# Three column tiles of gate weights split ahead, the second token half two tiles later, and the transfers and masks of the first FFN moved to its down stage

## The chip, the cores and the metric

The kernel runs on one core of a Trainium2 chip. The metric is the device time of one execution in microseconds (us), as the median of several runs. The engines are TensorE (PE in the profile; PEld is its weight load), VectorE (DVE), ScalarE (ACT), GpSimd (POOL) and SyncE (SP), each with an instruction stream of its own that it works off in order. SP's queue issues most transfers between memory and the chip; POOL issues the accumulating ones, each of which is an instruction in POOL's stream.

## The reference, cut to what matters

A decoder trunk with two layers on a sequence of 1024 tokens with 1024 features. Each layer is an FFN, a mixer and a second FFN, with a normalisation before and after each:

```
def swiglu(x, wg, wu, wd):
    return (jax.nn.silu(x @ wg) * (x @ wu)) @ wd

for layer in range(DEPTH):                       # DEPTH = 2
    f = swiglu(rmsnorm(h, ffn_pre_g[layer, 0]), ffn_w_gate[layer, 0], ffn_w_up[layer, 0], ffn_w_down[layer, 0])
    h = h + 0.5 * rmsnorm(f, ffn_post_g[layer, 0])
    m = rmsnorm(h, mix_pre_g[layer])
    m = hybrid_mixer(m, ...) if layer % 2 == 0 else stick_breaking(m, ...)
    h = h + rmsnorm(m, mix_post_g[layer])
    f = swiglu(rmsnorm(h, ffn_pre_g[layer, 1]), ffn_w_gate[layer, 1], ffn_w_up[layer, 1], ffn_w_down[layer, 1])
    h = h + 0.5 * rmsnorm(f, ffn_post_g[layer, 1])
```

The FFN's inner width is D_FF = 1408, eleven column tiles of 128. All is float32.

## The kernel before

**Stages.** Six stages follow one another: FFN, mixer, FFN, and the same in layer 1. The tokens are held as two halves of 512. Float32 products are made from two parts of each operand: a rounded one (fp32r) and the rest. A split is one ACT instruction (`L336` for weights, `L276` for others, CAST) and one DVE subtraction (`L337`, `L277`); a product is three matmuls (`mm3`, `L287` to `L289`). The large products use Strassen's scheme, so they need sums and differences of blocks of the operands.

**The gate and up products (`gu`).** Loop 1 runs over the eleven column tiles `c` of the gate weights. For each it loads the tile (`rawt`), splits its two halves (`wq`: `w0`, `w1`) and makes a quarter product of four times three matmuls, `w0` with the first token half (`quarter`, into `pa`); ACT copies the result to `ph`. The other quarter product (`a12`, with `w1`) runs a tile or two later, accumulates in the same bank, and ACT applies Silu to it (`L414`). At the tiles 2 to 5 `second_half` transposes the rows of the second token half on PE (`xps`, `L327`, eight transposes per call), which ACT copies out (`xr`, `L329`); at the tiles 4 to 7 `combos` makes the sums of Strassen's scheme on DVE (`L388` to `L397`). `pin` keeps the matmuls of the first six tiles in the order of the program; elsewhere a scheduler sets each engine's order when the kernel is built. Loop 2 runs over the eleven tiles again with the remaining five quarter products (`pb`, `pc`, `pd`, the last two used twice), the weight combinations made on POOL (`blocks`, `L421` to `L424`).

**Jobs.** `jobs` are steps on POOL's queue that a later stage needs: sums of weight blocks in memory, made by transfers that copy or accumulate (`Blocks.sums`, line `L82`), and, in the first FFN, the masks of the mixer (`mask_steps`, `L168` to `L187`). In the first FFN `job(0)` issues three steps in each tile of loop 1 after the third: 8 of masks and 16 of the sums `vsum`, for the value projection of the mixer. `job(1)` issues the sums for the down products (`dsum`) and for the mixer's output projection (`wsum`) in loop 2, as do the later FFNs for theirs.

**The down stage (`down_strassen`).** Seven products (`da` to `de`) of row tiles; each needs rows from memory (`rawd`) and splits. POOL makes the sums of `ph` (`L715`, `L725`). Then comes the epilogue of each token half: the residual rows `h` are loaded, the square sum goes from ACT (`junk`, `ss`) by DVE (`ms`, `L232`) to POOL, which makes its inverse root (`rs`, `L234`), and DVE scales the rows (`L248`). They go into the next stage's transposes.

**What is split ahead.** `first_weights` is called at the end of each stage, before the epilogue of the second token half, and gives `begun_w`, the next stage's first split weights: for an FFN column tile 0, two splits (`gate_weights(..., 0)`). The raw buffers (`rp`) are four, those of split weights (`wp`) six; both are shared by all the stages.

Of the kernel before, what the change touches and what calls it, by code (L numbers as in the profile page):

```python
# [24 lines left out]
NF = DFF // P  # L25
# [64 lines left out]
class Trunk:  # L90
# [263 lines left out]
    def gu(self, cx, wg, wu, A, xn1, gname, gi, jobs, begun):  # L354
# [11 lines left out]
        def second_half(part):  # L366
            R.update(self.make_raw(xn1, gname, gi, xr, [part, part + 4], pin))
            if part < 3:
                return
            self.hctx.close()  # L370
            self.foctx.close()
            rows["sx"] = self.dyn(s4, "sx", 4, side="right")
            rows["t2"] = self.dyn(s4, "t2p", 2, side="right")
# [23 lines left out]
            tt(out=a21, in0=a21, in1=lo(j + 4), op=ALU.add)  # L397

        ph, second = [], []
        pin = self.tc.keep_in_program_order  # L400
        paces = 3, -(-len(jobs[1]) // NF)

        def job(loop):
            for f in jobs[loop][:paces[loop]]:
                f()
            del jobs[loop][:paces[loop]]


        def a12():

# [5 lines left out]
        def blocks(c):  # L416
# [7 lines left out]
            gt(out=b21, in0=b21, in1=t2, op=ALU.subtract)  # L424
            return {"t1": b11, "t2": t2, "t3": b12, "t4": b21, "b22": b22}

        for c in range(NF):

            self.pin_mm = pin if c < 6 else None
            h = [self.ph.tile([P, TB], F32, name="ph%d" % tb, tag="ph") for tb in range(2)]  # L430
            w0, w1 = begun if begun and c == 0 else self.gate_weights(wg, c)
            ps = self.acc.tile([P, TB], F32, name="pa", tag="acc")
            self.quarter(ps, w0, A[0:4], True, True)
            nc.scalar.copy(out=h[1], in_=ps)
            while len(second) > (c < 8):
                a12()
            second.append((ps, w1, h))
            ph.append(h)
            if 2 <= c <= 5:
                second_half(c - 2)  # L440
            if 4 <= c <= 7:
                combos(c - 4)
            if c > 2:
                job(0)

        B = blocks(0)
        W = [self.split_w(B[n]) for n in ("t2", "t3")]
# [8 lines left out]
        for c in range(NF):  # L456
            h = ph[c]
            if c:
                B = blocks(c)
            pb = self.acc.tile([P, TB], F32, name="pb", tag="acc")  # L460
            pc = self.acc.tile([P, TB], F32, name="pc", tag="acc")
            pd = self.acc.tile([P, TB], F32, name="pd", tag="acc")
            if c == NF - 1:
                pe = self.acc.tile([P, TB], F32, name="pe", tag="acc")
                pf = self.acc.tile([P, TB], F32, name="pf", tag="acc")
            u2 = h[1]
            last = c == NF - 1
            self.quarter(pb, W[0] if c == 0 else self.split_w(B["t2"]), S[2], True, True)
            tt(out=u2, in0=pb, in1=u2, op=ALU.add)
            self.quarter(pc, W[1] if c == 0 else self.split_w(B["t3"]), S[3], True, True)  # L470
            c22 = tm.tile([P, TB], F32, name="c22", tag="c22")
            tt(out=c22, in0=pc, in1=u2, op=ALU.add)  # L472
            self.quarter(pd, W[2] if c == 0 else self.split_w(B["t1"]), S[1], True, True)
            c21 = tm.tile([P, TB], F32, name="c21", tag="c21")
            c12 = tm.tile([P, TB], F32, name="c12", tag="c12")
            if last:

                self.quarter(pe, self.split_w(B["t4"]), A22, True, True)
                self.quarter(pf, self.split_w(B["b22"]), S[4], True, True)
                tt(out=c12, in0=pd, in1=u2, op=ALU.add)  # L480
                tt(out=c21, in0=pe, in1=c22, op=ALU.add)
                tt(out=c22, in0=pd, in1=c22, op=ALU.add)
                nc.scalar.activation(out=c21, in_=c21, func=AF.Silu)
                tt(out=c12, in0=pf, in1=c12, op=ALU.add)
            else:
                tt(out=c22, in0=pd, in1=c22, op=ALU.add)
                w4, w3 = self.split_w(B["t4"]), self.split_w(B["b22"])
                self.quarter(pc, w4, A22, False, True)
                tt(out=c21, in0=pc, in1=u2, op=ALU.add)
                nc.scalar.activation(out=c21, in_=c21, func=AF.Silu)  # L490
                self.quarter(pd, w3, S[4], False, True)
                tt(out=c12, in0=pd, in1=u2, op=ALU.add)
            tt(out=h[0], in0=h[0], in1=c12, op=ALU.mult)
            tt(out=h[1], in0=c21, in1=c22, op=ALU.mult)
            if c > NF // 2:
                self.down_sums(ph, c - 1 - NF // 2)
            job(1)
        tmp.close()
        s4.close()
        return ph  # L500
# [110 lines left out]
    def ffn(self, l, f, x0, xn1, hsrc, hdst, last):  # L611
        a = self.a
        wg, wu, wd = a["ffn_w_gate"][l, f], a["ffn_w_up"][l, f], a["ffn_w_down"][l, f]
        cx = ExitStack()
        self.ph = self.dyn(cx, "ph", 2 * NF)
        self.s1 = []

        sums = lambda *sets: [step for steps in zip(*[B.sums(T) for B, T in sets]) for step in steps]
        down = self.down_blocks(l, f), self.wd[l, f]
        jobs = [], []  # L620
        if l + f == 0:
            jobs = self.mask_steps() + sums((self.value_blocks(0), self.tv)), sums(down, (self.out_blocks(0), self.td))
        elif l == 0:
            jobs = [], sums(down, (self.value_blocks(1), self.tv))
        elif f == 0:
            jobs = [], sums(down)
        ph = self.gu(cx, wg, wu, x0, xn1, "ffn_pre_g", 2 * l + f, jobs, self.begun_w)
        self.open_fo()
        pg = self.load_pg(a["ffn_post_g"][l, f])
        nxt = ("mix_pre_g", l) if f == 0 else ("ffn_pre_g", 2 * (l + 1))  # L630
        r = self.down_strassen(wd, self.wd[l, f], ph, pg, hsrc, hdst, None if last else nxt)
        cx.close()
        self.hctx.close()
        return r
# [13 lines left out]
        gt(out=z, in0=x, in1=z, op=ALU.subtract)  # L648
        self.s1.append(s1)

    def down_strassen(self, w, T, ph, pg, hsrc, hdst, nxt):
        nc = self.nc
        tt = nc.vector.tensor_tensor
        gt = nc.gpsimd.tensor_tensor
# [68 lines left out]
            tt(out=u2[t], in0=pb[t], in1=u2[t], op=ALU.add)  # L723
        for j in range(KH):
            gt(out=ph[j + KH][0], in0=ph[j][0], in1=ph[j + KH][0], op=ALU.subtract)  # L725

        cp = [pair("c22") for _ in range(2)]
        c22 = [cp[t // 2][:, t % 2] for t in range(NTT)]
# [5 lines left out]
        for t in range(NTT):  # L734
            c = fo[t][:, C[1]]
# [4 lines left out]
        a, b, ks = last_k(1, 1)  # L740
# [7 lines left out]
        for t in range(NTT):  # L748
            c = fo1[t][1]
# [896 lines left out]
    def build(self):  # L1646
        a = self.a
        self.ot = [[self.dram.tile([P, S], F32, name="otd%d_%d" % (l, k)) for k in range(KD)] for l in range(2)]
        self.vd = self.dram.tile([S, D], F32, name="vrows")

        self.sd = [self.dram.tile([P, 4 * TB], F32, name="osum%d" % j) for j in range(3)]
        self.tv, self.td = [{n: self.dram.tile([4 * P, TB], F32, name="%s%d" % (nm, n)) for n in (1, 2, 3, 4)}
                            for nm in ("vsum", "wsum")]
        self.wd = {(l, f): {n: self.dram.tile([NF // 2 * P, TB], F32, name="dsum%d%d_%d" % (l, f, n))
                            for n in (1, 2, 3, 4)} for l in range(2) for f in range(2)}
        self.gg = [self.dram.tile([P, S], F32, name="ggd%d" % h) for h in range(4)]
        for h in self.xn0:
            self.normed(h, h)
        x0 = self.make_first_x(self.xn0, "ffn_pre_g", 0, self.xp)
        x1 = self.first_x(1)  # L1660
        for h in x1:
            self.normed(h, h)
        src = a["x"][0]
        n = 0
        self.begun_w = self.pin_mm = None
        stages = [(l, step) for l in range(2) for step in ("f0", "mix", "f1")]
        firsts = [(lambda l=l: self.row_weights(lambda j: self.value_blocks(l).src(j, 0))) if step == "mix" else
                  (lambda l=l, f=int(step[1]): self.gate_weights(a["ffn_w_gate"][l, f], 0)) for l, step in stages]
        for l in range(2):
            for step in ("f0", "mix", "f1"):  # L1670
                self.first_weights = (firsts + [None])[stages.index((l, step)) + 1]
                last = l == 1 and step == "f1"
                dst = self.out[0] if last else self.new_h(n)
                n += 1
                if n == 2:
                    self.gate_consts()
                if step == "mix":
                    x0, x1 = self.mixer(l, x0, x1, src, dst)
                else:
                    x0, x1 = self.ffn(l, int(step[1]), x0, x1, src, dst, last)  # L1680
                src = dst
        self.foctx.close()
        self.fctx.close()
# [28 lines left out]
```

## Time and profile before

| what | value |
|---|---|
| median of 3 runs (lowest, highest) | 2486.64 us (2486.34, 2493.13) |
| the profiled execution | 2488.17 us, span 2486.2 us |
| TensorE clock granted, mean | 0.985 |
| DVE, ACT, POOL busy | 74%, 46%, 29% of the span |
| first PE work of loop 1 in the four FFNs (`pa`) | 16.6, 937.4, 1284.9, 2140.1 us |
| first PE work of loop 2 (`pb`) | 89.8, 1015.6, 1358.5, 2217.5 us |
| first PE work of the down stage (`da`) | 251.0, 1170.2, 1514.9, 2368.9 us |

The profile is of one execution; its times count from the start of the span. A row of a timeline gives the start in us, the duration in us, the engine, the line, the operation, what it writes and reads, and, in brackets, how long the engine was idle before it and what ended that. Rows that follow one another on PE overlap, since matmuls are pipelined. A row of the waits gives the engine and line that waited, what it waited for, then the us in total, the number of times and the longest. A row of a table of stretches gives the stretch, its length, the busy us of PE, PEld, DVE, ACT and POOL with the number of instructions, the granted clock, the busy share of the transfer engines and GB/s.

### The profile page before, as it was taken

To read this page: it belongs to the slowest core of one execution; us is meant where nothing else is said; L and a number is where in the kernel's file an instruction comes from. 1 tells how busy PE (TensorE), PEld (TensorE's weight loads), DVE (VectorE), ACT (ScalarE), POOL (GpSimd) and SP (SyncE) were. 2 spreads that over 40 slices of the span, in tenths; PEclk is the share of its full clock that TensorE was granted. 3 is DMA by queue.
4 is the path that set the end of the run, shared out by engine and by line. 5 is a ranking of instruction groups with operands and counts; after the bars stand their busy time and mean duration, and the time that the engine had idled before them with its cause. 6 is when DMAs were issued, how large, how long until landed. Compare 5 with 4: busy or idle time off the path is not lost. (4 is left out here: it accounts for less than half of the span.)

```text
span 2486.2 us, 31734 instructions
## 1 busy us (share of the span) xinstructions
PE 2352.8 (95%) x11165; PEld 1925.0 (77%) x11165; DVE 1840.1 (74%) x2877; ACT 1141.2 (46%) x2285; POOL 723.4 (29%) x729
## 2 busy tenths in 40 slices
PE   7999999999888898999989999999999999799998
PEld 6778877777677776877768878778888878588886
DVE  7768789387577778678688677785767677786777
ACT  6323456332466666423456225463333345652343
POOL 3547210011011111567022563110332430234520
PEclk9999999999999998999999999999999999899999
DMA  8867444411112463767454743355574244532234
GB/s 240 229 154 187 141 148 155 143 52 68 60 60 77 150 222 108 194 151 180 140 184 125 162 118 123 122 167 180 126 185 104 90 131 163 176 85 76 73 110 170
DMA packets 278407, 343.64 MB, mean 138 GB/s; under 512 B 13972, under 2 KB 190312, under 8 KB 277736
## 3 DMA queue, kind: packets, MB, share of 16 engines
q1 hardware_dynamic: 251352, 261.39, 33.6%
q0 software_dynamic: 26896, 80.22, 14.2%
q8 instruction: 88, 1.44, 0.2%
q14 instruction: 71, 0.58, 0.1%
HBM read 292.28 MB, written 124.78 MB: 168 GB/s over the span
## 5 line engine op out<-in xcount | busy, mean ns | idle before, releaser
L234 POOL TENSOR_TENSOR rs<-ms,nhalf 128x1 f32<-128x1 f32 (+1 forms) x136 | 103.7, 769 | 839.6 <-DVE ms L232 728.7
L336 ACT CAST wq<-rawt 128x512 fp32r<-128x512 f32 x264 | 163.3, 622 | 362.6 <-PE pc L289 181.9
L337 DVE TENSOR_TENSOR wq<-rawt,wq 128x512 fp32r<-128x512 f32 x264 | 246.5, 938 | 41.9 <-ACT wq L336 37.9
L276 ACT CAST hl<-rawd 128x512 fp32r<-128x512 f32 x212 | 130.7, 620 | 212.0 <-PE dc L289 63.9
L277 DVE TENSOR_TENSOR hl<-rawd,hl 128x512 fp32r<-128x512 f32 x212 | 155.4, 737 | 81.6 <-ACT hl L276 81.5
L287 PE MATMUL pps<-hl,wh 128*128 128x512 f32 x512 | 209.3, 409 | 1.4 <-ACT k L966 1.2
L288 PE MATMUL pps<-hl,wh 128*128 128x512 f32 x512 | 203.6, 398 | 0.0
L289 PE MATMUL pps<-hl,wl 128*128 128x512 f32 x512 | 202.9, 396 | 0.0
L421 POOL TENSOR_TENSOR rawt<-rawt 128x512 f32<-128x512 f32 x44 | 65.7, 1494 | 342.7 <-DMA rawt<-in_ffn_w_up_dram 287.0
L287 PE MATMUL pa<-hl,wq 128*128 128x512 f32 x352 | 143.1, 407 | 5.8 <-ACT wq L336 3.2
L289 PE MATMUL pa<-hl,wq 128*128 128x512 f32 x352 | 141.0, 401 | 8.1 <-DVE wq L337 8.1
L287 PE MATMUL pc<-hl,wq 128*128 128x512 f32 x336 | 133.0, 396 | 12.7 <-DVE c L472 11.8
L288 PE MATMUL pa<-hl,wq 128*128 128x512 f32 x352 | 140.5, 399 | 0.0
L289 PE MATMUL pc<-hl,wq 128*128 128x512 f32 x336 | 133.3, 397 | 0.0
L288 PE MATMUL pc<-hl,wq 128*128 128x512 f32 x336 | 133.3, 397 | 0.0
L288 PE MATMUL pd<-hl,wq 128*128 128x512 f32 x336 | 131.3, 391 | 0.0
L289 PE MATMUL pd<-hl,wq 128*128 128x512 f32 x336 | 131.2, 391 | 0.0
L287 PE MATMUL pd<-hl,wq 128*128 128x512 f32 x336 | 131.1, 390 | 0.0
L1076 DVE TENSOR_TENSOR_SCAN a<-a,zero 128x128 f32<-128x128 f32 (+3 forms) x64 | 90.2, 1409 | 46.5 <-POOL a L1073 46.2
L983 PE MATMUL z<-k,q 128*128 128x512 f32 (+2 forms) x480 | 113.6, 361 | 9.5 <-ACT k L966 4.3
L287 PEld LDWEIGHTS pps<-hl,wh 128*128 128x128 f32 x512 | 97.7, 191 | 21.5 <-ACT k L966 2.6
L289 PEld LDWEIGHTS pps<-hl,wl 128*128 128x128 f32 x512 | 97.5, 191 | 21.1
(359 smaller groups left out, 6642.0 us busy)
## 6 DMA issues: line engine op xcount, KB each, us to landing
rawt<-in_ffn_w_gate_dram SPq DMA_DIRECT2D x88, 512.0 KB, 4.0
dsum<-in_ffn_w_down_dram POOLq DMA_DIRECT2D x48, 640.0 KB, 8.0
rawt<-in_ffn_w_up_dram SPq DMA_DIRECT2D x44, 512.0 KB, 4.2
rawd<-dsum SPq DMA_DIRECT2D x80, 256.0 KB, 2.7
hres<-h SPq DMA_DIRECT2D x40, 512.0 KB, 2.7
h<-hres SPq DMA_DIRECT2D x40, 512.0 KB, 4.6
rawd<-in_ffn_w_down_dram SPq DMA_DIRECT2D x76, 256.0 KB, 2.7
dsum<-dsum POOLq DMA_DIRECT2D x16, 640.0 KB, 5.7
```

Of the source, the lines that this page charges most:

```text
L234: nc.gpsimd.tensor_tensor(out=rs, in0=ms, in1=self.nhalf.to_broadcast([P, n]) if n > 1 else self.nhalf, op=ALU.pow)
L276: nc.scalar.copy(out=t[:, 0], in_=src)
L277: nc.vector.tensor_tensor(out=t[:, 1], in0=src, in1=t[:, 0].bitcast(F32), op=ALU.subtract)
L287: pin(nc.tensor.matmul(ps, lhsT=ah, rhs=bh, start=first, stop=False, skip_group_check=more))
L288: pin(nc.tensor.matmul(ps, lhsT=ah, rhs=bl, start=False, stop=False, skip_group_check=more))
L289: pin(nc.tensor.matmul(ps, lhsT=al, rhs=bh, start=False, stop=last, skip_group_check=more))
L336: nc.scalar.copy(out=w[:, 0], in_=src)
L337: nc.vector.tensor_tensor(out=w[:, 1], in0=src, in1=w[:, 0].bitcast(F32), op=ALU.subtract)
L421: gt(out=b11, in0=b12, in1=b11, op=ALU.subtract)
L983: nc.tensor.matmul(z[:, :wide], lhsT=lhs[:, i * P:(i + 1) * P], rhs=rhs[:, c0:c0 + wide], start=j == 0, stop=j == len(passes) - 1 and not ...
L1076: nc.vector.tensor_tensor_scan(out=ra, data0=ra, data1=self.zero1.to_broadcast([P, n]), initial=1.0, op0=ALU.mult, op1=ALU.add)
```

## The change

In loop 1 of every FFN the transposes of the second token half go from the tiles 2 to 5 to the tiles 4 to 7, the combinations from 4 to 7 to 5 to 8, the matmuls of eight tiles instead of six are kept in the order of the program, and the last quarter products wait one tile longer (`c < 9`). `first_weights` gives three column tiles, six splits, for an FFN. The masks and the sums `vsum` of the first FFN leave loop 1; they are issued in its down stage, after POOL's differences of `ph`, first the sums and then the masks.

```
         for c in range(NF):
-            self.pin_mm = pin if c < 6 else None
+            self.pin_mm = pin if c < 8 else None
...
-            w0, w1 = begun if begun and c == 0 else self.gate_weights(wg, c)
+            w0, w1 = begun.pop(0) if begun else self.gate_weights(wg, c)
...
-            while len(second) > (c < 8):
+            while len(second) > (c < 9):
                 a12()
             second.append((ps, w1, h))
             ph.append(h)
-            if 2 <= c <= 5:
-                second_half(c - 2)
             if 4 <= c <= 7:
-                combos(c - 4)
-            if c > 2:
-                job(0)
+                second_half(c - 4)
+            if 5 <= c <= 8:
+                combos(c - 5)
...
-            jobs = self.mask_steps() + sums((self.value_blocks(0), self.tv)), sums(down, (self.out_blocks(0), self.td))
+            jobs = sums(down, (self.out_blocks(0), self.td))
+            steps = sums((self.value_blocks(0), self.tv)) + self.mask_steps()
...
         for j in range(KH):
             gt(out=ph[j + KH][0], in0=ph[j][0], in1=ph[j + KH][0], op=ALU.subtract)
+        for f in steps:
+            f()
...
-                  (lambda l=l, f=int(step[1]): self.gate_weights(a["ffn_w_gate"][l, f], 0)) for l, step in stages]
+                  (lambda l=l, f=int(step[1]): [self.gate_weights(a["ffn_w_gate"][l, f], c) for c in range(3)])
+                  for l, step in stages]
```

The line numbers of `gu` fall by two or so. How the built program moves is shown at three places.

ACT at the end of the mixer of layer 0, into the second FFN's loop 1, before: the squares of the epilogue (`junk,ss<-h`), the Silu of tile 0 (`L414`) and then the copies of the second half's first two transposed blocks (`L329`).

```order
L414 ACTIVATE ph_8509<-pa 128x512
L243 ACTIVATE junk,ss<-h 128x1024
L336 CAST wq<-rawt 128x512
L243 ACTIVATE junk,ss<-h 128x1024 x2
L329 ACTIVATE xr<-xps,gcol 128x512 x2
```

The same place now (`L433` copies a first quarter product, `L412` is the Silu):

```order
L412 ACTIVATE ph_8525<-pa 128x512
L243 ACTIVATE junk,ss<-h 128x1024
L433 COPY ph_8587<-pa 128x512
L243 ACTIVATE junk,ss<-h 128x1024
L412 ACTIVATE ph_8541<-pa 128x512
L243 ACTIVATE junk,ss<-h 128x1024
L336 CAST wq<-rawt 128x512 x3
L433 COPY ph_8624<-pa 128x512
L336 CAST wq<-rawt 128x512
L412 ACTIVATE ph_8557<-pa 128x512
L329 ACTIVATE xr<-xps,gcol 128x512 x2
```

Two copies and two Silus, which each wait for a quarter product of PE, now stand ahead of the first transposed blocks, two of them between the squares of the epilogue; the splits of `wq` between the squares go behind the last. On DVE, at the same place, the two splits that stood between the last scalings (`L248`) go behind them in the same way.

DVE at the end of the second FFN of layer 0, into the first of layer 1, before: the last outputs of the down stage are scaled by the gain (`L700`), then the epilogue of the second half begins (`L571`, `L232`, `L580`).

```order
L337 TENSOR_TENSOR wq<-rawt,wq 128x512
L280 SCALAR_TENSOR_TENSOR hl<-xps,gcol,hl 128x512
L700 TENSOR_TENSOR fo_3_11254<-fo_3_11254,pg 128x512
L571 TENSOR_TENSOR s_11275<-fs_10221 128x1
L571 TENSOR_TENSOR s_11284<-fs_10222 128x1
L571 TENSOR_TENSOR s_11293<-fs_10223 128x1
L232 TENSOR_SCALAR ms<-s_11275 128x1
L232 TENSOR_SCALAR ms<-s_11284 128x1
L232 TENSOR_SCALAR ms<-s_11293 128x1
L571 TENSOR_TENSOR s_11302<-fs_10224 128x1
L337 TENSOR_TENSOR wq<-rawt,wq 128x512
L580 SCALAR_TENSOR_TENSOR h<-fo_0_11239,rs,h 128x512
```

And now:

```order
L337 TENSOR_TENSOR wq<-rawt,wq 128x512
L280 SCALAR_TENSOR_TENSOR hl<-xps,gcol,hl 128x512
L699 TENSOR_TENSOR fo_3_11254<-fo_3_11254,pg 128x512
L337 TENSOR_TENSOR wq<-rawt,wq 128x512 x4
L568 TENSOR_TENSOR s_11291<-fs_10221 128x1
L568 TENSOR_TENSOR s_11300<-fs_10222 128x1
L568 TENSOR_TENSOR s_11309<-fs_10223 128x1
L232 TENSOR_SCALAR ms<-s_11291 128x1
L232 TENSOR_SCALAR ms<-s_11300 128x1
L232 TENSOR_SCALAR ms<-s_11309 128x1
L568 TENSOR_TENSOR s_11318<-fs_10224 128x1
L337 TENSOR_TENSOR wq<-rawt,wq 128x512
```

Four splits of gate weights now stand ahead of the epilogue, which is unchanged behind them.

POOL in the first FFN, before: the rows end loop 1's transfers, and the weight combinations of loop 2 follow (the 25 mask instructions stand just ahead of these rows).

```order
L82 DMA vsum_132<-in_hyb_w_in_dram 256x512 x2
L82 DMA vsum_134<-in_hyb_w_in_dram 256x512 x2
L82 DMA vsum_133<-vsum_132 16x8192 x2
L82 DMA vsum_133<-in_hyb_w_in_dram 256x512 x2
L82 DMA vsum_135<-vsum_133 16x8192 x2
L82 DMA vsum_135<-in_hyb_w_in_dram 256x512 x2
L421 TENSOR_TENSOR rawt<-rawt 128x512
L422 TENSOR_TENSOR t_890<-rawt 128x512
```

Now the combinations come straight after the inverse roots of the first rows:

```order
L234 TENSOR_TENSOR rs<-ms,nhalf 128x1 x8
L419 TENSOR_TENSOR rawt<-rawt 128x512
L420 TENSOR_TENSOR t_837<-rawt 128x512
L421 TENSOR_TENSOR rawt<-rawt 128x512
L422 TENSOR_TENSOR rawt<-rawt,t_837 128x512
L82 DMA dsum_1_140<-in_ffn_w_down_dram 320x512
```

And the transfers stand in the down stage, between the last differences of `ph` (`L724`) and the masks, behind which the epilogue's `rs` follow:

```order
L724 TENSOR_TENSOR ph_746<-ph_428,ph_746 128x512
L82 DMA vsum_132<-in_hyb_w_in_dram 256x512 x2
L82 DMA vsum_134<-in_hyb_w_in_dram 256x512 x2
L82 DMA vsum_132<-in_hyb_w_in_dram 256x512 x2
L82 DMA vsum_134<-in_hyb_w_in_dram 256x512 x2
L82 DMA vsum_133<-vsum_132 16x8192 x2
L82 DMA vsum_133<-in_hyb_w_in_dram 256x512 x2
L82 DMA vsum_135<-vsum_133 16x8192 x2
L82 DMA vsum_135<-in_hyb_w_in_dram 256x512 x2
L168 MEMSET zero_2407 128x1
L170 MEMSET one_2409 128x1
```

What moved is the place of 16 transfers and the masks on POOL's queue, from ahead of loop 2's weight combinations to ahead of the first epilogue's roots.

More of the change, by code (lines that the diff above doesn't have):

```diff
@@ L399, in gu, with job @@
         ph, second = [], []
[L400 to L404, printed above, removed]
+        pace = -(-len(jobs) // NF)
+        def job():
+            for f in jobs[:pace]:
                 f()
-            del jobs[loop][:paces[loop]]
+            del jobs[:pace]
         def a12():
@@ L425, in blocks @@
             return {"t1": b11, "t2": t2, "t3": b12, "t4": b21, "b22": b22}
+        pin = self.tc.keep_in_program_order
         for c in range(NF):
-            self.pin_mm = pin if c < 6 else None
+            self.pin_mm = pin if c < 8 else None
             h = [self.ph.tile([P, TB], F32, name="ph%d" % tb, tag="ph") for tb in range(2)]
-            w0, w1 = begun if begun and c == 0 else self.gate_weights(wg, c)
+            w0, w1 = begun.pop(0) if begun else self.gate_weights(wg, c)
             ps = self.acc.tile([P, TB], F32, name="pa", tag="acc")
@@ L496, in gu @@
                 self.down_sums(ph, c - 1 - NF // 2)
-            job(1)
+            job()
         tmp.close()
@@ L619, in ffn @@
         down = self.down_blocks(l, f), self.wd[l, f]
-        jobs = [], []
+        jobs, steps = [], []
         if l + f == 0:
-            jobs = self.mask_steps() + sums((self.value_blocks(0), self.tv)), sums(down, (self.out_blocks(0), self.td))
+            jobs = sums(down, (self.out_blocks(0), self.td))
+            steps = sums((self.value_blocks(0), self.tv)) + self.mask_steps()
         elif l == 0:
-            jobs = [], sums(down, (self.value_blocks(1), self.tv))
+            jobs = sums(down, (self.value_blocks(1), self.tv))
         elif f == 0:
-            jobs = [], sums(down)
+            jobs = sums(down)
         ph = self.gu(cx, wg, wu, x0, xn1, "ffn_pre_g", 2 * l + f, jobs, self.begun_w)
@@ L630, in ffn @@
         nxt = ("mix_pre_g", l) if f == 0 else ("ffn_pre_g", 2 * (l + 1))
-        r = self.down_strassen(wd, self.wd[l, f], ph, pg, hsrc, hdst, None if last else nxt)
+        r = self.down_strassen(wd, self.wd[l, f], ph, pg, hsrc, hdst, None if last else nxt, steps)
         cx.close()
@@ L649, in down_sums, with down_strassen @@
         self.s1.append(s1)
-    def down_strassen(self, w, T, ph, pg, hsrc, hdst, nxt):
+    def down_strassen(self, w, T, ph, pg, hsrc, hdst, nxt, steps):
         nc = self.nc
```

## The prediction

> **What bounds the kernel now.** First the page: the span, and how much of it TensorE works.
>
> ```profile
> span 2486.2 us, 31734 instructions
> PE 2352.8 (95%) x11165; PEld 1925.0 (77%) x11165; DVE 1840.1 (74%) x2877; ACT 1141.2 (46%) x2285; POOL 723.4 (29%) x729
> ```
>
> TensorE (PE) is the bound, and 2486.2 - 2352.8 = 133 us is all its idle time. A change that only moves work can win from that time and from time at a lower clock, so I next asked the view of waits for PE around each FFN start (us in total, times, longest). The first two rows below came out alike, digit for digit, for 900 to 1000 us (mixer of layer 0 to its second FFN) and for 2090 to 2200 us (the same in layer 1); the third is of 900 to 1000 us alone, the fourth of 1180 to 1320 us (second FFN of layer 0 to first FFN of layer 1).
>
> ```profile
> PE xps L327 <- DVE ms L232: 8.3, 3, 5.6
> PE xps L327 <- DVE fo L248: 1.4, 1, 1.4
> PE xps L268 <- DVE hl L280: 2.3, 1, 2.3
> PE pa L289 <- DVE wq L337: 7.0, 2, 5.5
> ```
>
> At the mixers' ends PE stands before the transposes of the second token half (xps, L327), which wait for the normed rows; at the FFN's end it stands before gate products (pa) for want of split weights (wq, L337). The table of stretches shows what else these places cost: the columns are the busy us of each engine, then the granted clock.
>
> ```profile
> 940.00:962.00 22.00, 11.63 (x47) 8.48 (x47) 18.46 (x36) 13.12 (x26) 7.00 (x8) 0.78 0.44 150
> 1280.00:1307.00 27.00, 20.04 (x80) 15.76 (x79) 20.97 (x43) 15.39 (x32) 6.30 (x8) 0.87 0.58 182
> 2127.00:2164.00 37.00, 23.56 (x109) 18.89 (x108) 27.07 (x49) 22.55 (x46) 7.01 (x8) 0.86 0.57 173
> ```
>
> The clock falls to 0.78, 0.87 and 0.86 there. The timeline of PE at the first of the three:
>
> ```profile
> 955.67 0.45 PE L327 MATMUL xps<-ident,fo 128*128 128x128 f32 x1 [5.64 <-DVE ms L232]
> 961.15 1.33 PE L327 MATMUL xps<-ident,fo 128*128 128x128 f32 x5 [1.38 <-DVE fo L248]
> 962.13 0.78 PE L287 MATMUL pa<-hl,wq 128*128 128x512 f32 x1
> 969.38 1.03 PE L327 MATMUL xps<-ident,fo 128*128 128x128 f32 x8
> 970.17 0.47 PE L287 MATMUL pa<-hl,wq 128*128 128x512 f32 x1
> 975.74 1.03 PE L327 MATMUL xps<-ident,fo 128*128 128x128 f32 x8
> 1015.63 0.39 PE L287 MATMUL pb<-hl,wq 128*128 128x512 f32 x1
> ```
>
> From these I take the prices. PE stopped at 955.67 - 5.64 = 950.03. A group of eight transposes takes 970.17 - 969.38 = 0.79. A tile's two quarter products (24 matmuls) take 975.74 - 970.17 = 5.57 at full clock, but 969.38 - 962.13 = 7.25 just after the stop: 1.68 us more, the price of the fallen clock. The second loop begins at 1015.63 (pb).
>
> **Part 1: transposes and combinations at tiles 4 to 7 and 5 to 8.** PE now has two more tiles, 2 x 5.57 = 11.1 us of gate work, ahead of the first transposes. Whether these can run is seen on VectorE (DVE):
>
> ```profile
> 955.50 0.68 DVE L337 TENSOR_TENSOR wq<-rawt,wq 128x512 fp32r<-128x512 f32 x1
> 960.34 0.75 DVE L248 TENSOR_SCALAR fo<-h,rs 128x1024 f32<-128x1024 f32 x1 [0.44 <-POOL rs L234]
> 963.28 0.69 DVE L388 TENSOR_TENSOR s<-xr 128x512 f32<-128x512 f32 x1 [2.19 <-ACT xr L329]
> 995.61 0.69 DVE L397 TENSOR_TENSOR xr<-xr,hl 128x512 f32<-128x512 f32 x1
> ```
>
> The last normed row is there at 960.34 + 0.75 = 961.1. The two splits that DVE used to do between the norms now wait behind them, which leaves POOL's chain of rs as it was. By this order tile 4's first half is split at 955.50 + 0.68 = 956.2, where PE wants it at 950.03 + 5.57 = 955.6: 0.6 us lost. So the transposes start at 950.03 + 11.1 + 0.6 = 961.7, when the rows are ready, and end at 962.5, against 962.13 now, with 11.1 us more work behind them; the 1.68 us of low clock goes too, since no long stop is left. Gain 11.1 + 1.7 - 0.4 = 12.4 us, and the same at the mixer of layer 1, which waits alike: 24.8 us. What is late next is then DVE at the end of loop 1 (first rival).
>
> In the first FFN PE doesn't wait for the transposes, so their move itself gains nothing there; it takes 11 us from DVE's lead. Every stage then has 14 quarters of 2.79 and three groups of transposes, 41.4 us, from the first group's end to loop 2.
>
> **Part 2: three column tiles split ahead.** At the mixers' ends five of the six splits already stand ahead of the splits of xps in DVE's order; the sixth costs one 0.7 us instruction there and two earlier loads, ahead of or between those of h. PE's 2.3 us wait at that point (L268, above) stands behind those splits and their loads, so I bound this by a loss of 0.7 and a gain of 2 us each and take 0, since most of the splits keep their place. At the FFN-to-FFN boundary it is the part that acts:
>
> ```profile
> 1289.77 0.50 PE L289 MATMUL pa<-hl,wq 128*128 128x512 f32 x1 [1.51 <-DVE wq L337]
> 1298.24 0.79 PE L289 MATMUL pa<-hl,wq 128*128 128x512 f32 x1 [5.45 <-DVE wq L337]
> 1305.93 1.04 PE L327 MATMUL xps<-ident,xn 128*128 128x128 f32 x8
> 1289.03 0.69 DVE L337 TENSOR_TENSOR wq<-rawt,wq 128x512 fp32r<-128x512 f32 x1
> 1301.31 0.75 DVE L248 TENSOR_SCALAR xn<-h,rs 128x1024 f32<-128x1024 f32 x1 [0.44 <-POOL rs L234]
> ```
>
> Now four more splits stand on DVE ahead of the epilogue, 4 x 0.69 = 2.8 us at most. All six splits are then done before the norms, so the 5.45 us goes; the 1.51 us, which hangs on the third split (at 1289.03 now, hardly sooner then), I let stay. The 22 matmuls from 1298.24 to 1305.93 took 7.69 where 22 x 0.232 = 5.1 would do: 2.6 us of clock goes as well. Gain 8.1 us. The epilogue ends 2.8 us later, at 1301.31 + 0.75 + 2.8 = 1304.9; but the transposes are due only at 1305.93 - 8.1 + 11.1 = 1308.9, and that covers it. Without the extra gate work the 2.8 us would be PE's.
>
> **Part 3: transfers and masks out of the first gate loop.** POOL's timeline, and PE's stops that follow:
>
> ```profile
> 27.42 0.10 POOL L168 MEMSET zero<- 128x1 f32 x1
> 36.92 2.46 POOL L82 DMA_DIRECT2D vsum<-in_hyb_w_in_dram  x4
> 78.37 0.89 POOL L82 DMA_DIRECT2D vsum<-in_hyb_w_in_dram  x1 [0.46 <-DMA vsum<-vsum]
> 78.97 1.61 POOL L421 TENSOR_TENSOR rawt<-rawt 128x512 f32<-128x512 f32 x1
> 333.31 2.33 POOL L234 TENSOR_TENSOR rs<-ms,nhalf 128x1 f32<-128x1 f32 x3 [65.64 <-DVE ms L232]
> 83.13 0.50 PE L287 MATMUL pa<-hl,wq 128*128 128x512 f32 x1 [0.53 <-ACT ph L434]
> 86.93 0.50 PE L287 MATMUL pa<-hl,wq 128*128 128x512 f32 x1 [0.75 <-ACT ph L434]
> 100.11 0.47 PE L287 MATMUL pc<-hl,wq 128*128 128x512 f32 x1 [1.85 <-DVE c L472]
> ```
>
> Masks (36.92 - 27.42 = 9.5 us) and the 16 transfers with their waits (to 79.3, 42.3 us) hold POOL until 78.97, where the weight combinations of loop 2 (L421) start, behind which ACT and then PE are late: 0.53 + 0.75 + 1.85 = 3.1 us. Freed, POOL starts them when the weights have landed. I take 3.1 as won, less 1 us for DVE's lost lead, 2.1 us. In the down stage the 51.8 us stand ahead of rs, the first thing the epilogue needs from POOL; POOL idles 65.64 us there, so 13.8 us of margin hide them: cost 0. Their traffic beside the row loads I bound by 0 and by the 3.1 us of stops that PE had beside them in the first FFN, and take 0: the row loads of the down stage have four buffers of lead.
>
> [...] In the first loop DVE was 99% busy beside these transfers:
>
> ```profile
> 50.00:60.00 10.00, 10.00 (x50) 8.34 (x48) 9.93 (x17) 7.61 (x14) 1.02 (x2) 1.00 1.15 238
> ```
>
> and the chain still took 42.3 us. [...]
>
> **The sum.** 24.8 + 8.1 + 2.1 = 35.0 us, less 0.5 us in each of the three later FFNs for DVE being nearer to late: 33.5. The profiled execution took 2488.17 (span 2486.2 and 2.0 around it), 0.06% above the median 2486.64, so I subtract from the median: 2453 us.
>
> **The rivals.**
>
> *DVE becomes the bound at the end of loop 1 (2471 us).* The combinations ran 963.28 to 996.3 with no POOL beside them:
>
> ```profile
> 996.17 1.29 POOL L421 TENSOR_TENSOR rawt<-rawt 128x512 f32<-128x512 f32 x1 [35.86 <-DMA rawt<-in_ffn_w_up_dram]
> 83.87 3.26 DVE L337 TENSOR_TENSOR wq<-rawt,wq 128x512 fp32r<-128x512 f32 x2
> 87.06 6.89 DVE L277 TENSOR_TENSOR hl<-xr,hl 128x512 fp32r<-128x512 f32 x4
> 93.86 0.68 DVE L337 TENSOR_TENSOR wq<-rawt,wq 128x512 fp32r<-128x512 f32 x1
> ```
>
> With the splits two tiles ahead, the raw buffers are free sooner and POOL's four subtractions fall into the combinations. Beside POOL six DVE instructions took 3.26 + 6.89 = 10.15 us, alone 6 x 0.6 = 3.6 (the stretch of 50 to 60 us has 17 in 10 us). Four such subtractions, at the 1.61 us of the one at 78.97, are a burst of 6.4 us; that costs DVE about 6.4 x (1 - 3.6/10.15) = 4.1 us. DVE would finish at 996.3 + 0.4 for the later transposes + 0.6 for one more split + 4.1 = 1001.4, and loop 2 is due at 962.5 + 41.4 = 1003.9: 2.5 us of slack, so one burst is free; a second, or later weights, is not. At 4.5 us lost in each of four FFNs, 18 us: 2471.
> [...]
>
> *The second loops shorten as well (2445 us).*
>
> ```profile
> 90.00:250.00 160.00, 152.61 (x656) 123.56 (x655) 122.50 (x137) 46.79 (x76) 96.63 (x80) 0.99 0.74 180
> 1016.00:1170.00 154.00, 151.29 (x660) 123.27 (x659) 114.72 (x132) 46.36 (x75) 93.02 (x75) 1.00 0.74 178
> ```
>
> The first FFN's loop 2 idles 7.4 us, the second's, with as many transfers, 2.7. If the missing backlog of transfers is the cause, 4.7 - 1.85 = 2.9 us more is won; with 2 us at each mixer's end and no loss on DVE (1.5), 8.4: 2445.
>
> *The wait only moves, and the change doesn't do what it says (2484 us).* ACT now evicts tiles between the squares of the epilogue; if that or the order of DVE delays the norms by as much as PE gained, the stops stay and 2.1 are won.
>
> *Slower (2500 us).* The transfers on POOL's queue hold rs in the down stage. Margin 13.8; beyond it each us delays the norms, the product after them and all else. To lose, the chain must last 13.8 + 33.5 = 47 us longer than its 51.8, nearly twice; at 13 us past that, 2500. Against it speak the 42.3 us that it took beside the densest traffic of the kernel; for it, that the rows of its new place don't exist yet.
>
> **How the numbers follow.** Forecast 0.56, its own range 2447 to 2461; DVE 0.18; second loops 0.17; wait only moves 0.04; slower 0.03; the rest 0.02 spread. 0.3% is 7.5 us, about what a measurement of this kernel can tell from no change. Faster: 0.56 + 0.18 + 0.17 and half of the rest, 0.92; same 0.04; slower 0.04. The range runs from the second loops' case to near the DVE case, 2441 to 2470.
>
> **What would show it.** Right: no PE wait over 2 us before xps at the mixers' ends, clock near 1.0 there; loop 2 (first pb) 12 us sooner after the mixer; no wq wait at the FFN boundary; POOL's first L421 (then L419) near 70 us; rs in the first down stage waiting for ms, not for vsum. Wrong: PE waits at the first pb or pc of a loop 2 on DVE, with DVE instructions of 1.2 to 1.8 us ahead of it; or rs late behind vsum.

## The result and the profile after

The changed kernel takes 2460.43 us (median of 4 runs, 2454.63 to 2467.38) against 2486.49 of the kernel before: a ratio of 0.9891, 95% interval 0.9859 to 0.9923, so 26.1 us faster. In later rounds (e10 below) it took 2462.05 (ratio 0.9896, 0.9879 to 0.9912). The profiled execution was the fastest of the four: 2454.63 us, clock 0.992.

The head of its page; PE's idle time falls from 133 to 109.5 us and its busy time, for the same 11165 matmuls, by 9.5, while the mean granted clock rises from 0.985 to 0.992:

```profile
span 2452.8 us, 31750 instructions
PE 2343.3 (96%) x11165; PEld 1914.4 (78%) x11165; DVE 1853.7 (76%) x2877; ACT 1137.6 (46%) x2285; POOL 727.4 (30%) x729
```

The waits of PE from 900 to 1000 us, around the end of the mixer of layer 0. The stops before `xps` at L327 are gone, and the 2.3 us before L268 is 0.4:

```profile
PE pa L287 <- ACT ph L433: 1.8, 2, 1.2
PE od L287 <- DVE c L1618: 1.6, 3, 0.9
PE xps L268 <- DVE hl L280: 0.4, 1, 0.4
PE pa L289 <- DVE wq L337: 0.3, 1, 0.3
```

The table of stretches (busy us of PE, PEld, DVE, ACT, POOL, then the granted clock) at the same three places as in the prediction. Behind both mixers the clock is whole now; at the boundary from the second to the third FFN it is not:

```profile
936.00:958.00 22.00, 21.09 (x96) 16.95 (x95) 19.31 (x39) 16.62 (x33) 6.25 (x8) 1.00 0.35 121
1266.00:1304.00 38.00, 30.58 (x128) 24.56 (x127) 23.84 (x48) 20.79 (x42) 5.98 (x8) 0.91 0.49 151
2119.00:2141.00 22.00, 21.10 (x97) 16.91 (x96) 19.31 (x39) 16.49 (x33) 6.25 (x8) 1.00 0.35 121
```

What happens there is seen in PE's timeline, and then in ScalarE's:

```profile
1273.57 0.50 PE L289 MATMUL pa<-hl,wq 128*128 128x512 f32 x1 [1.04 <-DVE wq L337]
1278.47 0.39 PE L289 MATMUL pa<-hl,wq 128*128 128x512 f32 x1
1285.23 0.79 PE L287 MATMUL pa<-hl,wq 128*128 128x512 f32 x1 [6.38 <-ACT ph L433]
1289.24 0.63 PE L287 MATMUL pa<-hl,wq 128*128 128x512 f32 x1
1301.08 1.03 PE L327 MATMUL xps<-ident,xn 128*128 128x128 f32 x8
```

```profile
1276.17 0.62 ACT L336 CAST wq<-rawt 128x512 fp32r<-128x512 f32 x1 [2.70 <-PE pa L289]
1278.33 1.06 ACT L243 ACTIVATE junk<-h 128x1024 bf16<-128x1024 f32 x1 [1.53 <-DVE h L577]
1283.56 1.06 ACT L243 ACTIVATE junk<-h 128x1024 bf16<-128x1024 f32 x1 [1.34 <-issue]
1284.61 1.54 ACT L433 COPY ph<-pa 128x512 f32<-128x512 f32 x3
```

PE has made the first quarter products of three tiles by 1278.9 and wants to add the second one into the bank of tile 0. That bank must first be copied out, and ACT's copies of all three tiles (L433) stand behind the epilogue's four squares (L243), the last of which began only at 1283.56. ACT itself idles 2.70 us in front of a split and 1.53 and 1.34 us in front of squares meanwhile: it isn't busy, its queue is in the wrong order. The 5.45 us wait for `wq` became a 6.38 us wait for `ph`, with ten matmuls at half clock behind it (0.43 us apart up to 1289.7).

Stage by stage, in us, from the first matmuls of `pa`, `pb` and `da` in each profile (loop 1 is `pa` to `pb`, loop 2 `pb` to `da`; the mixer columns run from `da` of the first or third FFN to the next `pa`). Experiments are numbered as below:

| kernel | loop 1 of FFN 1, 2, 3, 4 | loop 2 of FFN 1, 2, 3, 4 | mixer 0, 1 |
|---|---|---|---|
| before | 73.2, 78.2, 73.6, 77.4 | 161.2, 154.6, 156.4, 151.4 | 686.4, 625.2 |
| changed | 72.7, 66.5, 75.1, 66.6 | 158.7, 154.6, 153.7, 151.6 | 685.6, 618.7 |
| changed, profile of e10 | 72.4, 66.6, 74.5, 66.6 | 160.1, 154.0, 155.1, 151.7 | 685.4, 622.2 |
| part 1 (e1) | 80.1, 70.8, 74.1, 70.8 | 154.5, 159.8, 152.8, 151.6 | 684.8, 626.2 |
| part 2 (e2) | 74.1, 77.2, 72.9, 77.6 | 162.9, 153.6, 157.2, 151.4 | 685.8, 624.7 |
| part 2 again (e8) | 76.9, 77.0, 74.2, 77.8 | 160.0, 153.9, 155.3, 151.3 | 681.3, 620.8 |
| part 3 (e5) | 70.9, 77.2, 73.8, 79.2 | 155.1, 153.8, 155.0, 151.3 | 685.3, 627.6 |
| parts 1 and 2 (e3) | 79.0, 66.7, 75.0, 66.7 | 154.9, 153.9, 153.8, 151.6 | 684.4, 622.4 |
| late squares (e4) | 72.9, 66.6, 67.8, 66.7 | 160.7, 155.3, 156.7, 151.6 | 683.4, 620.1 |
| and FFN 1 early (e9) | 71.0, 66.6, 67.8, 66.6 | 155.8, 155.3, 157.1, 151.6 | 682.4, 620.2 |

Behind the mixers loop 1 repeats within 0.2 us in all kernels that have parts 1 and 2. Elsewhere two profiles of one kernel differ more, by up to 2.8 us in loop 1 (the first FFN in e2 and e8), by up to 2.9 in a second loop and by up to 4.5 in a mixer. A term of 2 us can be read from loop 1 behind the mixers, hardly from the whole time.

### The profile page after: what moved, and what is told of

Same layout as the page of the kernel before. It is cut to its first block, busy times and chain, and to the rows that moved or that the text cites. A ratio compares the mean times of both kernels' runs of the same rounds, so it can differ in the third digit from the quotient of the medians.

```text
span 2452.8 us, 31750 instructions
## 1 busy us (share of the span) xinstructions
PE 2343.3 (96%) x11165; PEld 1914.4 (78%) x11165; DVE 1853.7 (76%) x2877; ACT 1137.6 (46%) x2285; POOL 727.4 (30%) x729
## 5 line engine op out<-in xcount | busy, mean ns | idle before, releaser
L337 DVE TENSOR_TENSOR wq<-rawt,wq 128x512 fp32r<-128x512 f32 x264 | 245.3, 935 | 33.0 <-ACT wq L336 28.9
L419 POOL TENSOR_TENSOR rawt<-rawt 128x512 f32<-128x512 f32 x44 | 65.5, 1489 | 364.8 <-DMA rawt<-in_ffn_w_up_dram 235.3
```

Of the source, the lines that this page charges most:

```text
L337: nc.vector.tensor_tensor(out=w[:, 1], in0=src, in1=w[:, 0].bitcast(F32), op=ALU.subtract)
L419: gt(out=b11, in0=b12, in1=b11, op=ALU.subtract)
```

## The experiments

The ratios are to the kernel before, timed in the same rounds.

**e1: part 1 alone.** The kernel before with, in short,

```
-            self.pin_mm = pin if c < 6 else None
+            self.pin_mm = pin if c < 8 else None
-            while len(second) > (c < 8):
+            while len(second) > (c < 9):
-            if 2 <= c <= 5: second_half(c - 2)
-            if 4 <= c <= 7: combos(c - 4)
+            if 4 <= c <= 7: second_half(c - 4)
+            if 5 <= c <= 8: combos(c - 5)
```

> The kernel before with part 1 alone: second-half transposes at tiles 4 to 7, combinations at 5 to 8, matmuls pinned up to tile 7; one tile of gate weights split ahead; masks and vsum stay in loop 1. Theory: part 1 stands by itself, since most splits of the next tiles already lay ahead in VectorE's order. Loop 1 (first pa to first pb) of both FFNs behind a mixer falls by the 11.6 us that the changed kernel showed, 78.2 to about 66.6 and 77.4 to about 66; the other two loops stay within 1.5 us. Time about 2486.5 - 23 = 2463 us (2461 to 2467). Rival: part 1 needs part 2, because PE now wants tiles 1 to 3 split while VectorE still norms the rows; then a wait for wq takes the place of the wait for xps, loop 1 falls by 6 us or less, and the time is 2474 or more.

Measured: 2476.08 us, ratio 0.9959 (0.9944 to 0.9973); the time is the rival's. Loop 1 behind the mixers fell by 7.4 and 6.6 us, not 11.6, and a little more than the rival's 6. PE's waits there, from 930 to 1007 us, show why:

```profile
PE xps L268 <- DVE hl L280: 3.0, 1, 3.0
PE pa L289 <- DVE wq L337: 2.7, 1, 2.7
```

With one tile split ahead PE comes to a quarter whose weights aren't fully split, and stops for 2.7 us. The clock adds to it: the matmuls from 953.0 to 956.4 us run 0.43 us apart. So part 1 reaches its full size only with part 2: in e3, which has both, loop 1 takes 66.7 us there, against 66.5 and 66.6 in the changed kernel. Loop 1 of the first FFN, with vsum still in it, got 7 us longer, and its second loop 7 us shorter, which neither theory had.

**e2 and e8: part 2 alone, in two measurements.** The kernel before with `begun.pop(0)` and three `gate_weights` in `first_weights`.

> The kernel before with part 2 alone: three tiles of gate weights split ahead, transposes still at tiles 2 to 5. Theory (formed from the changed kernel's trace): at the boundary from the second to the third FFN the 5.45 us wait for wq goes, and a wait of 5 to 7 us for ScalarE's copy of the first pa takes its place, because that copy stands behind the epilogue's four squares in ScalarE's order; behind the mixers PE starts 2 us sooner and waits 2 us longer for the normed rows. Time 2486 us, within 2.5. Rival, the prediction's own term: 5.45 us of wait and 2.6 us of low clock go at that boundary, 2486.5 - 8.1 = 2478 us.

> Part 2 alone a second time, for a profile of a usual run: 11 of its 12 times lay at 2474 to 2484 us, the profiled one at 2488.6. Theory: loop 1 of the four FFNs is as in the first profile (74, 77, 73 and 77.5 us, with a 6.3 us wait for ScalarE's copy of pa in the third), and what differs lies in the second loops of the first three FFNs, which were 162.9, 153.6 and 157.2. Rival: part 2 does gain at the boundary from the second to the third FFN in usual runs, and the third's loop 1 comes to 69 us or less.

Measured: 2479.96 us, ratio 0.9970 (0.9958 to 0.9982), and 2480.86, ratio 0.9984 (0.9971 to 0.9998): 0.02% to 0.4% faster, between the theory's time and the rival's. Loop 1 of the third FFN stays at 72.9 and 74.2 us, so the gain isn't made at the boundary from FFN to FFN. There the wait moved just as the theory said (waits of PE from 1275 to 1358 us of e2):

```profile
PE pa L287 <- ACT ph L434: 6.3, 1, 6.3
PE pa L289 <- DVE wq L337: 1.1, 1, 1.1
```

A gain is visible at the ends of the mixers, where PE's waits for L268 are 0.4 us instead of 2.3 and 3.1 while the waits for the rows are within 0.4 us of what they were; so the epilogue came sooner along with PE, which neither theory had. The guess of e8 that two profiles of this kernel would differ in the second loops alone was wrong too: of 8.7 us between them 8.4 lie in the mixers, 4.6 in the second loops, and loop 1 takes 4.1 back. What makes a mixer 4 us longer in one execution than in the next was not followed up.

**e5: part 3 alone.** The kernel before with `mask_steps` and the sums `vsum` issued in the down stage.

> The kernel before with part 3 alone: masks and vsum issued in the first down stage, nothing else changed. Theory: the moved work matters in the first FFN alone, and there the second loop, which waits for transfers, takes back most of what the first loop gives: first pa to first da falls from 234.4 us by 2 to 3, the first down stage with its mixer (first da to the next pa, 686.4 us before) stays within 1 us, and the time is about 2485 us (2481 to 2488), too small a step to tell from no change with certainty. Rival: with vsum in the down stage its 16 transfers and GpSimd's queue cost the 3.1 us of the bound, first da to next pa rises to 689 and the time is 2488 or more.

Measured: 2476.80 us, ratio 0.9963 (0.9950 to 0.9977), 7.1 us by the medians. The first FFN fell from 234.4 to 226.0 us, 2.3 in loop 1 and 6.1 in loop 2; the mixer column from 686.4 to 685.3. The direction is the theory's, the size some three times its own (8.4 us in the first FFN against 2 to 3).

**e3: part 3 undone.** The changed kernel with masks and vsum back in loop 1, `for f in early[:3]` from tile 3.

> The changed kernel with part 3 undone: masks and vsum back in loop 1 of the first FFN, three a tile from tile 3, ahead of what the queue did there before. Theory: part 3 is worth the 2.1 us of the prediction, in the first FFN's second loop (158.7 us from first pb to first da goes back to 161), and cost nothing in the down stage: 2460.4 + 2 = 2462.5 us. Rival: the transfers cost something in the first down stage (bounded there at 3.1 us), then this kernel is as fast as the changed one or up to 1 us faster.

Measured: 2464.39 us, ratio 0.9919 (0.9901 to 0.9936): 2.3 to 4 us slower than the changed kernel's two medians, about the theory's size, though the intervals overlap. The first FFN takes 233.9 us against 231.4 and 232.5. The place is not the theory's: loop 1 is longer and loop 2 shorter. What part 3 clears away is seen in three timelines of the first FFN's loop 1 (POOL, ACT, PE):

```profile
78.36 0.89 POOL L82 DMA_DIRECT2D vsum<-in_hyb_w_in_dram  x1 [0.90 <-DMA vsum<-vsum]
78.96 1.61 POOL L419 TENSOR_TENSOR rawt<-rawt 128x512 f32<-128x512 f32 x1
81.97 0.62 ACT L336 CAST wq<-t 128x512 fp32r<-128x512 f32 x1 [7.76 <-POOL t L420]
90.18 0.80 PE L287 MATMUL pa<-hl,wq 128*128 128x512 f32 x1 [5.73 <-ACT ph L433]
```

POOL gets to the weights of loop 2 only when the last vsum transfer is issued; ACT stands 7.76 us in front of the split of `t`, with copies of `pa` queued behind it, and PE then waits for one of these (ACT loses another 2.87 us to DVE's `s`, L394, ahead of it). The 5.7 us and the low clock behind them (matmuls 0.43 us apart up to 95.5 us) make loop 1 79.0 us long, but loop 2 gives 4 to 5 of it back.

**e4: the squares behind the copies.** The changed kernel; at the boundary from the second to the third FFN alone, in short:

```
 # epilogue of the second token half
-        for t in range(NTT):
-            self.normed(hs[t], xns[t], act)
+        self.late = lambda: [self.normed(hs[t], xns[t], act, pin) for t in range(NTT)]
 # gu, behind the copy of a tile's pa
             nc.scalar.copy(out=h[1], in_=ps)
+            if gi == 2 and c == 2:
+                self.late()          # the squares are kept behind the copies
```

> The changed kernel with one thing moved: at the boundary from the second to the third FFN alone, the four squares of the last epilogue's norm are issued behind ScalarE's copies of the first three pa tiles, not ahead of them. Theory: the 6.4 us wait of PE for ScalarE's ph (L433) and the ten matmuls at half clock behind it come from that order alone. The wait falls below 1 us, loop 1 of the third FFN falls from 75.1 to about 67 us, and the time from 2460.4 to about 2452 (2449 to 2455). Rival: what PE waits for is the epilogue as such; with the copies early the wait moves to the splits of tile 3 or to the normed rows at the transposes, loop 1 stays within 2 us of 75 and the time within 2 us of the changed kernel's.

Measured: 2452.56 us, ratio 0.9864 (0.9845 to 0.9882); loop 1 of the third FFN 67.8 us. Each number is the theory's but the wait, which fell to 1.2, not below 1. PE's timeline and ACT's, then the stretch that answers to the one above:

```profile
1280.98 0.50 PE L287 MATMUL pa<-hl,wq 128*128 128x512 f32 x1 [1.20 <-ACT ph L433]
1294.72 1.03 PE L327 MATMUL xps<-ident,xn 128*128 128x128 f32 x8
1280.35 1.56 ACT L433 COPY ph<-pa 128x512 f32<-128x512 f32 x3
1281.78 1.08 ACT L243 ACTIVATE junk<-h 128x1024 bf16<-128x1024 f32 x1
```

```profile
1266.00:1304.00 38.00, 35.75 (x164) 29.09 (x163) 30.70 (x59) 25.75 (x51) 5.31 (x8) 1.00 0.55 172
```

The last square now begins at 1285.35, and the transposes wait for nothing: they come 24.6 us after the first `pa` (31.9 in the changed kernel). Against the changed kernel 7.3 us of loop 1 are won, and 7.9 us by the medians; of the 8.1 us that the prediction gave part 2, 5.8 now show in loop 1 (73.6 us before), and ACT's order had kept them.

**e6: transfers where there were none.** The changed kernel, with the 32 sums of the second FFN also issued in the second loop of the fourth:

```
-        elif f == 0:
-            jobs = sums(down)
+        else:
+            jobs = sums(down) if f == 0 else sums((down[0], self.wd[1, 0]), (self.value_blocks(1), self.tv))
```

> The changed kernel with extra transfers: the fourth FFN's second loop, which had none of them, issues the same 32 sums that the second FFN's second loop issues (into tables that nobody reads any more). Theory: the 1 to 7 us that PE waits for VectorE's c22 in the second loops of the first three FFNs, other in every run, come from the load on the DMA queues (their share 0.74, 0.74 and 0.55; in the fourth 0.28 with no wait): the weights of the next tile land late at GpSimd. Then the fourth's second loop goes from 151.6 us, where six kernels had it within 0.2, to 153 to 157, its DMA share to about 0.74, and waits of pc for VectorE's c appear there. Rival: the waits come from VectorE's or GpSimd's own load, which is about the same in all four; then it stays at 151.6 to 152.

Measured: 2468.84 us, ratio 0.9926 (0.9908 to 0.9944); the loop takes 159.1 us instead of 151.6, more than the theory's 157. The median time from issue to landing of its weight tiles, in the changed kernel and then in e6:

```profile
rawt<-in_ffn_w_up_dram SPq DMA_DIRECT2D x9, 512.0 KB, 4.2
```

```profile
rawt<-in_ffn_w_up_dram SPq DMA_DIRECT2D x9, 512.0 KB, 7.0
```

One step of the chain in e6 (POOL, DVE, PE):

```profile
2207.14 1.29 POOL L419 TENSOR_TENSOR rawt<-rawt 128x512 f32<-128x512 f32 x1 [9.82 <-DMA rawt<-in_ffn_w_up_dram]
2211.54 1.78 DVE L490 TENSOR_TENSOR ph<-ph,c 128x512 f32<-128x512 f32 x1
2213.24 1.77 DVE L491 TENSOR_TENSOR ph<-c,c 128x512 f32<-128x512 f32 x1
2217.45 0.47 PE L287 MATMUL pc<-hl,wq 128*128 128x512 f32 x1 [2.22 <-DVE c L469]
```

The tile lands late, POOL's combinations begin late, and they then lie beside DVE's sums, which take 1.78 instead of 0.69 us; PE waits behind them. This loop had no such wait in the profiles of the kernel before, the changed one and e1 to e4, so the added sums are enough to cause such waits. Whether it is their traffic or their place on POOL's queue e6 doesn't separate: POOL's busy time rises as well, from 75.5 us (2183 to 2335 us of the changed kernel) to 95.7 (2184 to 2345 of e6).

**e7: the second vsum in a down stage.** The kernel of e4 with the sums of `value_blocks(1)` moved from the second FFN's loop 2 into `steps` of the third FFN.

> The kernel of the late squares, with the second vsum table (for layer 1's mixer) moved out of the second FFN's second loop into the down stage of the third FFN, as part 3 did with the first. Theory: the second FFN's second loop gets the DMA load of the third's (0.74 to about 0.5) and loses 1 to 2 us of its 154.6 to 155.5; GpSimd's chain ends before the norms of the third down stage want rs, so first da to the next pa there (about 620 us) stays within 1.5 us. Time 2451 us against the 2452.6 of the late squares (2447 to 2454). Rival: the longer queue in the third down stage holds rs, and the time is 2455 or more.

Measured: 2452.83 us, ratio 0.9869 (0.9855 to 0.9883), the same as e4. The second FFN's loop 2 came out at 158.0 us, not lower, with 3.9 us of waits for `c` at a DMA share of 0.53, against 155.3 us, 3.2 and 0.74 in e4. So the load of the queues isn't the only thing that sets these waits, and what else does stays open; by the theory the down stage with its mixer was to stay within 1.5 us; it is 3 us longer in this profile (623.4 against 620.1), as much as mixers differ anyway.

**e9 and e10: part 1 taken back in the first FFN, and the changed kernel again.** e9 is e4 with the transposes of the first FFN at tiles 2 to 5, its combinations at 4 to 7, pins up to tile 5; e10 is the changed kernel as it is.

> The kernel of the late squares, with part 1 taken back in the first FFN alone: there the second-half transposes stand at tiles 2 to 5 and the combinations at 4 to 7 again. Theory: part 1 has nothing to gain in the first FFN and costs VectorE's lead there, which loop 2 pays for; part 3 alone had 226.0 us from the first pa to the first da, the four profiled kernels with parts 1 and 3 had 231.4 to 233.6. It falls to 226 to 228, and the time from 2452.6 to about 2447 us (2444 to 2450). Rival: the 226.0 was one good profile of a loop whose transfers land otherwise in every run; then the first FFN stays at 231 or more and the time within 2 us of 2452.6.

> The changed kernel itself once more, timed in the same rounds as the kernel of the early first FFN. Theory: 2460 us (2457 to 2464), with loop 1 of the third FFN at 75 us (the 6.4 us wait for ScalarE's ph), which is in the order of the instructions, and the first FFN at 231 to 234 us; the spread from run to run, some 10 us, is that of the second loops and the mixers. Rival: the 75 us was a mishap of one profile; then loop 1 comes out at 69 us or less.

Measured: 2446.46 us for e9, ratio 0.9832 (0.9812 to 0.9851), and 2462.05 for e10; the first FFN takes 226.8 and 232.5 us, loop 1 of the third 67.8 and 74.5. Both theories hold, and e9 is the fastest kernel of the study, 15.6 us below the changed one in the same rounds. POOL's second set of weight combinations in the first FFN and the load ahead of it, in e10 and then in e9:

```profile
78.84 0.37 SPq L351 DMA_DIRECT2D rawt<-in_ffn_w_up_dram  x1
84.71 1.63 POOL L419 TENSOR_TENSOR rawt<-rawt 128x512 f32<-128x512 f32 x1 [9.66 <-DVE wq L337]
```

```profile
72.19 0.37 SPq L351 DMA_DIRECT2D rawt<-in_ffn_w_up_dram  x1
76.11 1.28 POOL L419 TENSOR_TENSOR rawt<-rawt 128x512 f32<-128x512 f32 x1 [0.92 <-DMA rawt<-in_ffn_w_up_dram]
```

With the combinations at tiles 5 to 8 DVE splits the last gate tiles late, and these hold the four raw buffers: SP's queue waits for a split (`wq`, L337; 21.7 us in three waits from 60 to 85 us in the first profile of the changed kernel) and issues the load 6.7 us later. POOL's next combinations begin 8.6 us later and then fall on DVE's last splits of the rows (e10):

```profile
84.53 5.78 DVE L277 TENSOR_TENSOR hl<-xr,hl 128x512 fp32r<-128x512 f32 x4
```

which take 1.4 us each here and 0.6 alone. DVE is through with loop 1 at 95 us in e10, at 88 in e9.

## Why the prediction was right, and where it was not

The forecast was 2453 us with a range of 2441 to 2470; the median is 2460.4, inside the range and at the end of the likeliest case's own (2447 to 2461). The profiled execution won 2486.2 - 2452.8 = 33.4 us, almost the 33.5 of the sum, but that is luck: its terms were off by up to 10 us in both directions, and the other three executions were 4 to 13 us slower. By the table, the terms 24.8, 8.1, 2.1 and -1.5 came out at 22.5 (loop 1 behind the mixers), -1.5 (loop 1 at the boundary from FFN to FFN), 3.0 (the first FFN) and 2.5 (the other second loops); 7.3 more lie in the mixer columns, where the sum had nothing, and -0.4 elsewhere. In e10's profile the mixer columns give 4.0.

**Part 1, 24.8 us: right in place and nearly in size.** Loop 1 behind the mixers fell by 11.7 and 10.8 us, 22.5 together; PE has no stop over 1.2 us there, the clock is 1.00, and the rows are ready before the transposes. The first `pb` came 66.5 us after the first `pa` instead of 78.2. But e1 shows that 8.5 us of it are only there because the tiles 1 and 2 are split ahead as well.

**Part 2 at the mixers' ends, taken as 0 within -0.7 and +2: the wrong end.** I read DVE's order, found most splits in their place and left it at that. The waits at L268 fell by 1.9 and 2.7 us (from 2.3 and 3.1 to 0.4, in e2 with part 2 alone); the 3.1 stood in the view of 2090 to 2200 us, and the bound was taken from the row of 900 to 1000 alone. Another 4.3 and 4.2 came in loop 1 through part 1 (70.8 to 66.5 and 66.6). The 12.4 of part 1 had these last in it under another name.

**Part 2 at the boundary from FFN to FFN, 8.1 us: the step that failed.** "All six splits are then done before the norms, so the 5.45 us goes" was right; loop 1 still got 1.5 us longer. The step looked at the one engine that PE waited for, DVE, and not at the next that it would wait for. The row was in the profile before, of ScalarE's timeline:

```profile
1297.94 1.05 ACT L434 COPY ph<-pa 128x512 f32<-128x512 f32 x2
```

Two copies already stood behind the last square, although PE had begun `pa` at 1284.9; PE's wait for `wq` up to 1298.24 hid it. A cover that is taken away uncovers what lay under it. The rival "the wait only moves" saw that copies and squares share ACT's queue ("ACT now evicts tiles between the squares of the epilogue"), but had the copies delay the norms, not the squares the copies, and got 0.04. e4 turns the loss of 1.5 into a gain of 5.8 in loop 1 by moving nothing but these squares, so the cause is shown.

**Part 3, 2.1 us: near in size, by two errors that cancel.** The gain alone, taken as 3.1, is 7.1 us (e5); the cost of part 1 in the first FFN, taken as 1, is 6 (below). Within the change 2 to 4 are left (e3). I had counted three stops of PE, 3.1 us; e3 shows that the late weights do more, through ACT's order, and e5 that they cost most in loop 2. That the down stage pays nothing was right: POOL's timeline there has the sums, the masks, and then a wait for `ms` in front of the roots, not for vsum:

```profile
264.60 2.27 POOL L82 DMA_DIRECT2D vsum<-in_hyb_w_in_dram  x4
310.14 0.88 POOL L82 DMA_DIRECT2D vsum<-in_hyb_w_in_dram  x1 [1.79 <-DMA vsum<-vsum]
318.82 0.84 POOL L187 TENSOR_SCALAR_AFFINE_SELECT lm<-lm 128x64 f32<-128x64 f32 x1
330.03 2.87 POOL L234 TENSOR_TENSOR rs<-ms,nhalf 128x1 f32<-128x1 f32 x3 [10.36 <-DVE ms L232]
```

The chain took 46.4 us there against 42.3 in loop 1, and 10.4 us of margin were left of the forecast 13.8. DVE was busy for 31.6 of these 46.4 us (264.6 to 311.0), and in loop 1 before for 33.0 of 42.4 (36.9 to 79.3); the forecast's 99% hold for 10 us of that. POOL's first L419 began here at 66.9 us, forecast near 70:

```profile
66.86 1.68 POOL L419 TENSOR_TENSOR rawt<-rawt 128x512 f32<-128x512 f32 x1 [39.35 <-DVE xr L391]
```

**The first FFN under part 1: named, and priced at 1.** "It takes 11 us from DVE's lead" was the cost, and 1 us for it was put into part 3. e9 shows 6. It ends as the first rival has it, with POOL's subtractions on DVE's last splits, but they fall there because POOL's weights come later, not sooner; the rival spread it over four FFNs at 4.5 us, and it came in the one where part 1 had nothing to win. In the second and fourth FFN loop 2 took 154.6 and 151.6 us (154.6 and 151.4 before), so the 1.5 us set aside for DVE there were not needed.

**Second loops shorter as well.** Not as a rule: 158.7 and 160.1 in the changed kernel's two profiles of the first FFN, 161.2 before. The gain that the rival had in mind is there, though, when part 1 doesn't take it away: 155.1 with part 3 alone (e5), and 155.8 in e9.

## What to carry to other kernels

Before a wait is taken away, ask of every engine that the waiting one needs next when it will be ready, not only of the one it waits for now; instructions that are late but hidden are in the profile, with their times. An engine that idles can be the one that is late, as ACT was in e3 with 7.76 us of idle time and the wanted copy in its queue: what counts is what stands ahead of the wanted instruction in its queue. A move that pays at one boundary should be made there alone, and tried without the places that have nothing to gain.

## What the hardware showed that was not expected

PE lost nearly as much behind a stop of 2.7 us (e1) as behind the one of 6.38 in the changed kernel: eight matmuls 0.43 us apart instead of ten, where 0.23 is the full rate. Behind one of 1.2 us (e4) it lost nothing: the granted clock is 1.00 from 1280 to 1290 us. After the 2.69 us stop in e1 it ran at full rate for 1.5 us, and then eight matmuls came 0.43 us apart, for 3.4 us:

```profile
951.46 0.50 PE L289 MATMUL pa<-hl,wq 128*128 128x512 f32 x1 [2.69 <-DVE wq L337]
952.49 0.40 PE L287 MATMUL pa<-hl,wq 128*128 128x512 f32 x1
953.01 0.63 PE L289 MATMUL pa<-hl,wq 128*128 128x512 f32 x1
955.57 0.63 PE L289 MATMUL pa<-hl,wq 128*128 128x512 f32 x1
956.37 0.39 PE L288 MATMUL pa<-hl,wq 128*128 128x512 f32 x1
```

The length of the stop alone doesn't decide. In the profile before, a stop of 1.87 us in the second loop of the third FFN is followed, 1.0 us after its end, by eight matmuls 0.43 us apart, for 3.4 us:

```profile
1480.19 0.47 PE L287 MATMUL pc<-hl,wq 128*128 128x512 f32 x1 [1.87 <-DVE c L472]
1481.19 0.62 PE L288 MATMUL pc<-hl,wq 128*128 128x512 f32 x1
1484.17 0.59 PE L289 MATMUL pc<-hl,wq 128*128 128x512 f32 x1
1484.60 0.40 PE L287 MATMUL pd<-hl,wq 128*128 128x512 f32 x1
```

Behind the one of 1.85 us that ended at 100.11, in the second loop of the first FFN, the matmuls come 0.22 to 0.31 us apart for the next 9 us. What decides no run here shows.
